# A two-layer decoder trunk on one core: the first four weight tiles side by side, the bias write in four transfers, two small reorderings

## The chip, the cores and the metric

One core of a Trainium2 chip runs the whole program. The metric is device time in microseconds (us). TensorE (PE) multiplies, VectorE (DVE) and ScalarE (ACT) do the elementwise work, SyncE (SP) issues nearly all DMA transfers, GpSimd (POOL) builds a few masks. Engines run their own instruction lists in order and wait for each other by semaphores.

## The reference

x is 512 tokens by 2048. Two layers, each `x = x + mixer(rmsnorm(x))`, then a last rmsnorm.

- Layer 1: one projection gives q, k, v, a gate g (16 heads of 128 each) and a small indexer (16 heads of 64). The indexer scores every causal key, `score = sum_h relu(iq_h . ik) * iw_h`; each query keeps its best 128 keys; softmax attention runs over those, with logits that carry a learned bias by distance (32 buckets per head). The result times `silu(g)` goes through the output projection.
- Layer 2: one projection gives z, x/B/C and dt; a causal convolution of four taps with SiLU; a chunked state-space scan over 64 heads with states carried between chunks of 128 tokens; times `silu(z)`, rmsnorm, output projection.

All matrices are fp32.

## The kernel before

Every dense product keeps fp32 accuracy by three matmuls: a weight block and an activation block are each split into a high part (rounded to fp32r, by ACT: `wh`, `xh`) and a low rest (by DVE: `wl`, `xl`), and PE adds `wh*xh + wh*xl + wl*xh`.

Work is cut into **units**. A dense tile gives 128 output columns; with 2048 input rows it is four units of four blocks of 128 rows, so a unit is 4 steps of three matmuls, twelve in all. The order of everything is written by hand: a main loop goes through the units, and a step counter (`now`, four per unit) wakes generators ("threads") whose `yield n` means "n steps later". Three units (`LEAD`) ahead of PE the loop emits the splits of the coming unit: ACT's `wh` at step 0, DVE's `wl` at step 2. Since every engine works in program order, an instruction that waits holds up all that stands behind it on its engine.

Weights come in transfers of 1 MB, one tile each (`raw<-wa`), into three buffers. `load_next` issues the next one when the last `wl` of a tile has been emitted, which is 12 units before PE needs it. All these loads stand in SP's list, between the small transfers.

The units of layer 1 in order, as the change finds them: the first five indexer tiles `wa[0]` to `wa[4]` (units 0 to 19, quarter by quarter: unit 0 is the first four blocks of tile 0, unit 1 those of tile 1, and so on); indexer tiles 5 to 7 (units 20 to 31); `wai`, the indexer's key (32 to 35); twelve gate tiles g0 to g11 (36 to 83); then v, q and k by heads.

At the start SP issues x's first four blocks and the first quarter of each of the five tiles; ACT issues the rest (`load_early_thread`). `prep_x` splits a block of x. `square_x` sums the squares of x for the first rmsnorm.

`bias_setup` (from unit 40) makes, with one small matmul `r`, a table of 16 heads by 384 distances, 16 partitions high, in the tile `rs`. One transfer then writes each head's row 128 times to a scratch in DRAM, each time one element further on, so that later a skewed read gives each head's bias block (`bias_load`, first used far later, at unit 100):

```
dst = bias_scr.rearrange("h (p m) -> h p m", m=385)[:, :, 0:384]
sy.dma_start(out=dst, in_=rs[:HA, None, :384].to_broadcast([HA, P, 384]))
```

From unit 36 on, `index_thread` puts the indexer's `dots` matmuls between the units, ACT takes their relu, DVE sums them to `score`, and `topk_thread` (DVE, lines 446 and 447) finds the best 128 keys.

`head_thread` does one head's attention: logits for query blocks 3, 2, then 1 and 0 (tiles `la`, `lb`, `lc`; the probabilities of block 0 are in a part of `lb`, scaled last, line 548); then transposes (`ptp`, line 558) in three groups of key blocks, each split by ACT (`pth`) and DVE (`ptl`); then the products with v (`av`).

`pairs_thread` (layer 2) makes the states of two head pairs: `xd2` split by ACT and DVE (`xd2l`), some steps later the six matmuls `st`, then `yo`.

Of the kernel before, what the change touches and what calls it, by code (L numbers as in the profile page):

```python
# [16 lines left out]
P = 128  # L17
# [25 lines left out]
def kernel(  # L43
# [27 lines left out]
    def T(name, dt=F32):  # L71
        return slots.tile([P, S], dt, tag="u", name=name)
# [46 lines left out]

    def cols_load():  # L120
        sy.dma_start(out=cols, in_=cols_in)
        ve.tensor_scalar(out=cols[:, C_CW:C_D], in0=cols[:, C_CW:C_D], scalar1=0.5, scalar2=None, op0=ALU.mult)

    def col(base, k):
# [32 lines left out]
    def spawn(gen, delay=1):  # L157
        threads.append([now[0] + delay, gen])
# [15 lines left out]
    class Dense:  # L174
        def __init__(self, src, ncol, nk, operand, evac, t0=0, t1=S, packed=False, early=None,
                     order=None, keep=(), given=None):
            self.order = list(order or range(nk // 4))
            self.keep, self.given = keep, given
            self.src, self.ncol, self.nk, self.operand, self.evac = src, ncol, nk, operand, evac
            self.t0, self.t1, self.packed, self.early = t0, t1, packed, early  # L180
            self.raw = {}
            self.w = {}

        def load(self, c, eng=sy):
# [3 lines left out]
            n = 4 * self.ncol  # L188
            for u in range(4):
                self.raw[4 * c + u] = r[:, u * n : (u + 1) * n]  # L190

        def load_unit(self, u, eng):
            r = T("rawu")
            eng.dma_start(out=r, in_=self.src[:, 4 * u : 4 * u + 4].rearrange("p k j -> p (k j)"))
            self.raw[u] = r

        def split_hi(self, u):
            n = 4 * self.ncol
# [9 lines left out]
        def split_lo(self, u):  # L208
            if self.given and u in self.given.keep:
                return  # L210
            hi, lo = self.w[u][:2]
            sub(lo, self.raw.pop(u).rearrange("p (k j) -> p k j", k=4), f(hi))
# [24 lines left out]
    class TokenMajor:  # L237
# [21 lines left out]
        def mm(self, u, b):  # L259
# [10 lines left out]
            if u == 15:  # L270
                run(self.evac(out, b))

    tiles = []
    units = []
    hooks = {}

    def dense(src, ncol, nk, operand, evac, **kw):
        d = Dense(src, ncol, nk, operand, evac, **kw)
        tiles.append(d)
        if d.early is None:  # L280
            for u in d.order:
                units.append((d, u))
        return d

    def at_unit(idx, fn):
        hooks.setdefault(idx, []).append(fn)
# [43 lines left out]

    xf, xhl = {}, {}

    def load_x(k, eng):
        xf[k] = T("x")
        eng.dma_start(out=xf[k], in_=xT[k])

    def prep_x(k):
        xhl[k] = yield from split_scaled("x", xf[k], col(C_NW0, k))
# [4 lines left out]
    def square_x():  # L343
        for k in range(KD):
            yield from sum0.push(xf.pop(k))
            yield 1
        yield 4
        yield from rms_chain(sum0.acc, D, True, after_rms0)
# [7 lines left out]
    def bias_setup():  # L356
        rel, oh = T("rel"), T("oh")
        sy.dma_start(out=rel[:32, :HA], in_=rel_in)
        sy.dma_start(out=oh[:32, :384], in_=onehot_in)
        yield 16  # L360
        r = PS("r")
        te.matmul(r[:HA, :384], rel[:32, :HA], oh[:32, :384], start=True, stop=True)
        rs, c0 = T("rs"), SM("c0", 1)
        ve.tensor_copy(out=c0[:HA], in_=r[:HA, 0:1])
        ve.tensor_scalar(out=rs[:HA, :384], in0=r[:HA, :384], scalar1=c0[:HA], scalar2=None, op0=ALU.subtract)
        dst = bias_scr.rearrange("h (p m) -> h p m", m=385)[:, :, 0:384]
        sy.dma_start(out=dst, in_=rs[:HA, None, :384].to_broadcast([HA, P, 384]))

    def bias_load(h):
        b = T("bias")  # L370
# [11 lines left out]
    def evac_iq(t):  # L382
        def go(ps):
            a, b = T("iqa", F32R), T("iqb", F32R)
            for q, h, l in ((a, slice(0, HI), slice(HI, P)), (b, slice(HI, P), slice(0, HI))):
                sc.copy(out=q[h, :384], in_=ps[h])
                yield HOP
                sub(q[l, :384], ps[h], f(q[h, :384]))
            iqhl[t] = (a, b)
        return go  # L390
# [117 lines left out]
    def head_thread(h):  # L508
# [40 lines left out]
            yield 1  # L549
        yield 2  # L550
        pt = {}
        for grp in ((0,), (1,), (2, 3)):
            ps = PS("ptp")
            n = 0
            hi, lo = T("pth", F32R), T("ptl", F32R)
            for j in grp:
                for i in range(j, NB):
                    te.transpose(ps[:, n + (i - j) * P : n + (i - j + 1) * P],  # L558
                                 prob[i][:, j * P : (j + 1) * P], ident)
                w = (NB - j) * P  # L560
                pt[j] = (hi[:, n : n + w], lo[:, n : n + w])
                n += w
            yield 2
            if 3 in grp:

                pt[3] = hi[:, 2 * P :]
                sc.copy(out=hi[:, :n], in_=ps[:, :n])
                yield HOP
                sub(lo[:, : 2 * P], ps[:, : 2 * P], f(hi[:, : 2 * P]))
                sub(hi[:, n:], ps[:, 2 * P : n], f(hi[:, 2 * P : n]))  # L570
            else:
                yield from split(hi[:, :n], lo[:, :n], ps[:, :n])
            yield 1
# [265 lines left out]
    def pairs_thread(p):  # L839
        bth, btl, ch, cl = state_in[p // 4]  # L840
        d2 = T("xd2")
        for e in range(2):
            yield from xdt_make(p + e, d2[:, 256 * e : 256 * e + 256])
        hi, lo = T("xd2h", F32R), T("xd2l", F32R)
        yield from split(hi, lo, d2)
        yield 8
        st = PS("st")[:, :256]
        blk = lambda a, s: a.rearrange("p (e c d) -> p c e d", e=2, c=2)[:, s]
        for s in range(2):
            ss = slice(s * P, (s + 1) * P)  # L850
            te.matmul(st, bth[:, ss], blk(hi, s), start=s == 0, stop=False)
            te.matmul(st, bth[:, ss], blk(lo, s), start=False, stop=False)
            te.matmul(st, btl[:, ss], blk(hi, s), start=False, stop=s == 1)
        sh, sl = T("sth", F32R)[:, :256], T("stl", F32R)[:, :256]
        yield 2
        yield from split(sh, sl, st)
        yield 5
        yo = PS("yo")
        for e in range(2):
            o, es = yo[:, 256 * e : 256 * e + 256], slice(e * P, (e + 1) * P)  # L860
            te.matmul(o, sh[:, es], ch[:, 256:], start=True, stop=False)
            te.matmul(o, sh[:, es], cl[:, 256:], start=False, stop=False)
            te.matmul(o, sl[:, es], ch[:, 256:], start=False, stop=True)
        t = T("yo")
        yield 2
        sc.copy(out=t, in_=yo)
        for e in range(2):
            yoff[p + e] = t[:, 256 * e : 256 * e + 256]
# [189 lines left out]
    def mark():  # L1058
        return len(units)

    EARLY_TILES = 5
    for t in range(8):
        dense(wa[t], P, 16, opA, evac_iq(t), t0=P, early=t if t < EARLY_TILES else None)
        if t == EARLY_TILES - 1:
            for u in range(4):
                for d in tiles:
                    units.append((d, u))
    dense(wai, 80, 16, opA, evac_idx)
    for h in range(12):
        dense(wa[8 + h], P, 16, opA, evac_g(h))  # L1070
# [33 lines left out]
    dense(wbo[KD - 1], P, 32, opO, evac_last(1), t0=256, order=range(7, -1, -1), given=first_half)  # L1104
    u_end = mark()

    at_unit(40, lambda: spawn(bias_setup(), 0))
    at_unit(17, lambda: spawn(square_x(), 0))
    at_unit(u_fill_a, lambda: spawn(og_convert_thread(), 0))
    at_unit(u_out_a - 2, lambda: [res_load(xT, j) for j in range(2)])  # L1110
    at_unit(u_b - 4, lambda: sy.dma_start(out=heads, in_=heads_in))
# [29 lines left out]
    def load_next(eng=sy):  # L1141
        if nxt_chunk[0] < len(chunks):
            d, c = chunks[nxt_chunk[0]]
            d.load(c, eng)
            nxt_chunk[0] += 1

    early = tiles[:EARLY_TILES]

    def load_early(u, eng):
        if u:  # L1150
            early[0].load_unit(u, eng)
        for k in range(4 * u, 4 * u + 4):
            load_x(k, eng)
            if k == 0:
                early[0].load_unit(u, eng)
            yield 1
        for d in early[1:]:
            d.load_unit(u, eng)
            yield 1

    def load_early_thread():
        for u in range(1, 4):
            yield from load_early(u, sc)
            yield 3
        load_next(sc)
        yield 8
        load_next(sc)
        yield 16
        load_next(sc)

    for _ in load_early(0, sy):
        pass

    def prep_x_thread():
        for k in range(4, KD):
            spawn(prep_x(k), 0)
            yield 3

    def split_now(i):
        d, u = units[i]  # L1180
        d.split_hi(u)
        d.split_lo(u)

    x0 = prep_x(0)
    next(x0)
    d0, u0 = units[0]
    d0.split_hi(u0)
    for _ in x0:
        pass
    d0.split_lo(u0)  # L1190
    for k in range(1, 4):
        for _ in prep_x(k):
            pass
    for i in range(1, LEAD):
        split_now(i)
    spawn(load_early_thread(), 0)
    spawn(prep_x_thread(), 3)
    at_unit(12, cols_load)

    for i in range(u_end):  # L1200
        j = i + LEAD
# [81 lines left out]
```

## Time and profile before

| | |
|---|---|
| device time, median of 3 runs | 2418.91 us (2417.77 to 2419.24) |
| the profiled execution's own time | 2418.09 us |
| span of its profile | 2416.4 us |
| PE busy | 2399.8 us, 99% |
| PE weight loads busy | 2016.2 us, 83% |
| DVE busy | 1582.5 us, 65% |
| ACT busy | 1072.4 us, 44% |
| granted PE clock | 0.999 of full speed |

The span runs from the first instruction to the last; 1.7 us of the execution's own time lie outside it. Matmuls are pipelined, so a matmul shown as 0.39 us follows the one before it after 0.23 us; a short wait shows as a longer distance between two starts rather than as idle time.

### The profile page before, as it was taken

To read this page: it belongs to the slowest core of one execution; us is meant where nothing else is said; L and a number is where in the kernel's file an instruction comes from. 1 tells how busy PE (TensorE), PEld (TensorE's weight loads), DVE (VectorE), ACT (ScalarE), POOL (GpSimd) and SP (SyncE) were. 2 spreads that over 40 slices of the span, in tenths; PEclk is the share of its full clock that TensorE was granted. 3 is DMA by queue.
4 is the path that set the end of the run, shared out by engine and by line. 5 is a ranking of instruction groups with operands and counts; after the bars stand their busy time and mean duration, and the time that the engine had idled before them with its cause. 6 is when DMAs were issued, how large, how long until landed. Compare 5 with 4: busy or idle time off the path is not lost.

```text
span 2416.4 us, 29873 instructions
## 1 busy us (share of the span) xinstructions
PE 2399.8 (99%) x11398; PEld 2016.2 (83%) x11398; DVE 1582.5 (65%) x2891; ACT 1072.4 (44%) x2134; POOL 1.2 (0%) x8
## 2 busy tenths in 40 slices
PE   9999999999999999999999999999999999999998
PEld 9878888888888888888888888888888888888887
DVE  6569466464654654358788888888888888433334
ACT  6433233333333433234556565565656566322222
POOL 0000000000000000000000000000000000000000
PEclk9999999999999999999999999999999999999999
DMA  6362322222222224433333333333334344333333
GB/s 223 103 130 88 107 93 74 92 90 90 94 79 93 82 105 142 146 122 130 122 108 119 118 122 126 127 127 106 124 107 142 112 149 157 127 114 100 101 113 109
DMA packets 83440, 278.54 MB, mean 115 GB/s; under 512 B 7744, under 2 KB 40928, under 8 KB 58208
## 3 DMA queue, kind: packets, MB, share of 16 engines
q1 hardware_dynamic: 78976, 266.41, 33.0%
q10 hardware_dynamic: 4320, 10.23, 1.2%
q8 instruction: 89, 1.46, 0.3%
q14 instruction: 55, 0.45, 0.1%
HBM read 258.32 MB, written 18.02 MB: 114 GB/s over the span
## 4 chain that ended last, share of the span: by engine, by line
PE 96%; DVE 2%; DMA 2%; issue 0%; ACT 0%; SPq 0%; DVEq 0%; ACTq 0%
PE acc L229 27%; PE acc L231 27%; PE acc L230 27%; PE acc L265 2%; PE acc L267 2%; PE acc L266 2%; DMA raw<-wa 2%; PE ptp L558 1%; PE y L917 1%; PE y L916 1%; PE xst L819 1%; PE sps L525 0%; PE sps L526 0%; PE sps L524 0%; PE av L588 0%; PE av L586 0%
## 5 line engine op out<-in xcount | busy, mean ns | idle before, releaser
L90 DVE TENSOR_TENSOR wl<-raw,wh 128x512 fp32r<-128x512 f32 (+1 forms) x788 | 528.7, 684 | 136.8 <-ACT wh L206 96.2
L206 ACT CAST wh<-raw 128x512 fp32r<-128x512 f32 (+1 forms) x724 | 427.0, 613 | 173.9 <-PE acc L230 100.1
L229 PE MATMUL acc<-x1h,wh 128*128 128x512 f32 x1280 | 503.4, 393 | 0.0
L230 PE MATMUL acc<-x1l,wh 128*128 128x512 f32 x1280 | 499.5, 390 | 0.0
L231 PE MATMUL acc<-x1h,wl 128*128 128x512 f32 x1280 | 499.2, 390 | 0.0
L229 PE MATMUL acc<-xh,wh 128*128 128x512 f32 (+2 forms) x912 | 353.5, 388 | 2.3 <-ACT wh L206 2.1
L231 PE MATMUL acc<-xh,wl 128*128 128x512 f32 (+2 forms) x912 | 349.6, 383 | 0.3
L230 PE MATMUL acc<-xl,wh 128*128 128x512 f32 (+2 forms) x912 | 348.8, 382 | 0.6 <-DVE xl L101 0.6
L231 PEld LDWEIGHTS acc<-x1h,wl 128*128 128x128 f32 x1280 | 240.4, 188 | 50.9
L229 PEld LDWEIGHTS acc<-x1h,wh 128*128 128x128 f32 x1280 | 240.8, 188 | 46.6
L230 PEld LDWEIGHTS acc<-x1l,wh 128*128 128x128 f32 x1280 | 240.9, 188 | 46.1
L229 PE MATMUL acc<-ygh,wh 128*128 128x512 f32 (+1 forms) x544 | 205.4, 378 | 0.0
L231 PE MATMUL acc<-ygh,wl 128*128 128x512 f32 (+1 forms) x544 | 205.0, 377 | 0.0
L230 PE MATMUL acc<-ygl,wh 128*128 128x512 f32 (+1 forms) x544 | 205.0, 377 | 0.0
L231 PEld LDWEIGHTS acc<-xh,wl 128*128 128x128 f32 (+1 forms) x912 | 170.6, 187 | 35.1 <-DVE wl L90 2.2
L229 PEld LDWEIGHTS acc<-xh,wh 128*128 128x128 f32 (+1 forms) x912 | 170.7, 187 | 31.8 <-ACT wh L206 2.6
L230 PEld LDWEIGHTS acc<-xl,wh 128*128 128x128 f32 (+1 forms) x912 | 171.0, 187 | 29.8 <-DVE xl L101 1.4
L231 PEld LDWEIGHTS acc<-ygh,wl 128*128 128x128 f32 x544 | 102.4, 188 | 18.8
L230 PEld LDWEIGHTS acc<-ygl,wh 128*128 128x128 f32 x544 | 102.4, 188 | 18.7
L229 PEld LDWEIGHTS acc<-ygh,wh 128*128 128x128 f32 x544 | 102.4, 188 | 18.5
L727 DVE SCALAR_TENSOR_TENSOR hh<-rw,cols,hh 128x511 f32<-128x511 f32 x144 | 107.4, 746 | 6.5 <-ACT hh L724 4.0
L887 ACT ACTIVATE bc<-bc,aloc 128x256 f32<-128x256 f32 (+1 forms) x256 | 102.8, 446 | 0.5
(295 smaller groups left out, 3316.1 us busy)
## 6 DMA issues: line engine op xcount, KB each, us to landing
raw<-wb SPq DMA_DIRECT2D x80, 1024.0 KB, 4.9
raw<-wa SPq DMA_DIRECT2D x48, 1024.0 KB, 4.9
raw<-wbo SPq DMA_DIRECT2D x33, 1024.0 KB, 4.8
bc<-r_scr SPq DMA_DIRECT2D x96, 256.0 KB, 6.1
raw<-wav SPq DMA_DIRECT2D x16, 1024.0 KB, 4.9
raw<-wao SPq DMA_DIRECT2D x16, 1024.0 KB, 5.4
yg_scr<-yy SPq DMA_DIRECT2D x24, 256.0 KB, 4.6
ygr<-yg_scr SPq DMA_DIRECT2D x24, 256.0 KB, 5.1
```

The lines of the kernel that those rows point to most:

```text
L90: ve.tensor_tensor(out=out, in0=a, in1=b, op=ALU.subtract)
L206: sc.copy(out=self.w[u][0], in_=self.raw[u].rearrange("p (k j) -> p k j", k=4))
L229: te.matmul(out[:m], w[0], xh[:, ts], start=first, stop=False)
L230: te.matmul(out[:m], w[0], xl[:, ts], start=False, stop=False)
L231: te.matmul(out[:m], w[1], xh[:, ts], start=False, stop=last)
L265: te.matmul(out, xh[:, bs], wh, start=u == 0, stop=False)
L266: te.matmul(out, xh[:, bs], wl, start=False, stop=False)
L267: te.matmul(out, xl[:, bs], wh, start=False, stop=u == 15)
L558: te.transpose(ps[:, n + (i - j) * P : n + (i - j + 1) * P], prob[i][:, j * P : (j + 1) * P], ident)
L727: ve.scalar_tensor_tensor(out=hh[:, d:], in0=rw[:, : S - d], scalar=col(C_CW, 4 * ct + 3 - d), in1=hh[:, d:], op0=ALU.mult, op1=ALU.add)
L819: te.transpose(ps[:, c * P : (c + 1) * P], xs[p][:, c * P : (c + 1) * P], ident)
L887: sc.activation(out=t3[:, e, a:b], in_=t3[:, e, a:b], func=AF.Relu, scale=-1.0, bias=aloc[:, s, 2 * p + e : 2 * p + e + 1])
```

## The change

Four things change.

1. The first four tiles are worked side by side (`FourTiles`). A unit is now one block of 128 rows of x against that block of all four tiles, so units 0 to 15 hold four tiles; the fifth tile becomes an ordinary one. SP issues all early loads, x block by x block: for the first four blocks a transfer of 128 partitions x 4 tiles x 128 columns (rows of 512 B), after that for four blocks at once, 1 MB (rows of 2 KB). ACT issues none. The number of units stays the same.
2. `bias_setup` starts four units earlier, and its write goes in four transfers of four heads, 24 steps (6 units) apart.
3. A head's transposes are done for key blocks (2, 3), then 1, then 0, instead of 0, 1, (2, 3).
4. The `st` matmuls come 10 steps after the split of `xd2`, not 8.

The loading of `cols` moves into the row of early loads, and its scaling to unit 20; `square_x` starts at unit 13, not 17.

```diff
+    class FourTiles:
+        def load(self, k):
+            load_x(k)
+            if k < 4:
+                self.raw[k] = T("rawu").rearrange("p (t j) -> p t j", t=4)
+                sy.dma_start(out=self.raw[k], in_=self.src[:4, :, k].rearrange("t p j -> p t j"))
+            elif k % 4 == 0:
+                r = raw_pool.tile([P, 16 * P], F32, tag="raw", name="raw").rearrange("p (t k j) -> p t k j", t=4, k=4)
+                sy.dma_start(out=r, in_=self.src[:4, :, k : k + 4].rearrange("t p k j -> p t k j"))
...
+        def split_hi(self, k):
+            self.x = prep_x(k)
+            next(self.x)
+            self.w[k] = [T("wh", F32R), T("wl", F32R)]
+            sc.copy(out=self.cut(self.w[k][0]), in_=self.raw[k])
...
+        def mm(self, k, t):
+            if k == 0 and t == 0:
+                self.acc = [PS("acc4")[:, : S - self.t0] for _ in range(4)]
...
+            te.matmul(self.acc[t], wh, xh, start=k == 0, stop=False)
+            te.matmul(self.acc[t], wh, xl, start=False, stop=False)
+            te.matmul(self.acc[t], wl, xh, start=False, stop=k == KD - 1)
...
@@ bias_setup
-        sy.dma_start(out=dst, in_=rs[:HA, None, :384].to_broadcast([HA, P, 384]))
+        for g in range(4):
+            hs = slice(4 * g, 4 * g + 4)
+            sy.dma_start(out=dst[hs], in_=rs[hs, None, :384].to_broadcast([4, P, 384]))
+            yield 24
@@ head_thread
-        for grp in ((0,), (1,), (2, 3)):
+        for grp in ((2, 3), (1,), (0,)):
@@ pairs_thread
-        yield 8
+        yield 10
...
-    at_unit(40, lambda: spawn(bias_setup(), 0))
-    at_unit(17, lambda: spawn(square_x(), 0))
+    at_unit(36, lambda: spawn(bias_setup(), 0))
+    at_unit(13, lambda: spawn(square_x(), 0))
...
+    for k in range(KD):
+        first.load(k)
+        if k == 11:
+            cols_load()
+    for _ in range(3):
+        load_next()
```

Where instructions stand now, at three places. First, SP's list at the bias write; `raw` is the next 1 MB weight tile (here the gate tiles g4, g5 and so on). Before:

```order
L187 DMA raw_1100<-wa 128x2048
L367 DMA bias_scr_118<-rs_1196 2048x1x384
L187 DMA raw_1211<-wa 128x2048
L187 DMA raw_1314<-wa 128x2048
L187 DMA raw_1424<-wa 128x2048
```

With the change:

```order
L414 DMA bias_scr_118<-rs_1057 512x1x384
L189 DMA raw_1083<-wa 128x2048
L189 DMA raw_1187<-wa 128x2048
L414 DMA bias_scr_118<-rs_1057 512x1x384
L189 DMA raw_1291<-wa 128x2048
L414 DMA bias_scr_118<-rs_1057 512x1x384
L189 DMA raw_1402<-wa 128x2048
L189 DMA raw_1530<-wa 128x2048
L414 DMA bias_scr_118<-rs_1057 512x1x384
L189 DMA raw_1658<-wa 128x2048
```

The one write of 2048 rows stood behind the load for g4 (raw_1100) and ahead of that for g5. Now four writes of 512 rows stand ahead of the loads for g4 (raw_1083), g6 (raw_1291), g7 (raw_1402) and g9 (raw_1658).

Second, PE's list at the transposes of the last head (la, lb and lc hold the probabilities). Before:

```order
L558 MATMUL ptp_7550<-ident_95,lb_7309 128x128
L558 MATMUL ptp_7550<-ident_95,lc_7310 128x128
L558 MATMUL ptp_7550<-ident_95,lb_7309 128x128
L558 MATMUL ptp_7550<-ident_95,la_7308 128x128
...
L586 MATMUL av_7664<-pth_7551,vh_6374 128x512
L587 MATMUL av_7664<-ptl_7552,vh_6374 128x512
```

With the change:

```order
L606 MATMUL ptp_7529<-ident_95,lb_7288 128x128
L606 MATMUL ptp_7529<-ident_95,la_7287 128x128 x2
...
L606 MATMUL ptp_7588<-ident_95,lb_7288 128x128
L606 MATMUL ptp_7588<-ident_95,lc_7289 128x128
L606 MATMUL ptp_7588<-ident_95,lb_7288 128x128
L606 MATMUL ptp_7588<-ident_95,la_7287 128x128
...
L634 MATMUL av_7643<-pth_7589,vh_6353 128x512
L635 MATMUL av_7643<-ptl_7590,vh_6353 128x512
```

The first group needed all four query blocks, block 0's part of lb among them; now it needs blocks 2 and 3 alone, and the group that needs all four comes last, just ahead of the product with v that reads it (ptp_7588 is split into pth_7589 and ptl_7590).

Third, SP's list at the very start (`rawu` is the weight data of one early unit). Before:

```order
L118 DMA nw_93<-cols 128x16
L335 DMA x<-xT 128x512
L194 DMA rawu<-wa 128x512
L335 DMA x<-xT 128x512 x3
L194 DMA rawu<-wa 128x512 x4
```

With the change:

```order
L118 DMA nw_93<-cols 128x16
L380 DMA x<-xT 128x512
L283 DMA rawu<-wa 128x4x128
L380 DMA x<-xT 128x512
L283 DMA rawu<-wa 128x4x128
L380 DMA x<-xT 128x512
L283 DMA rawu<-wa 128x4x128
```

x and weights now alternate, block by block, and a weight transfer has 512 rows of 512 B where it had 128 rows of 2 KB.

## Rows read from the trace of the kernel before

**Rows 1.** The page: the span and the engines' busy time.

```profile
span 2416.4 us, 29873 instructions
PE 2399.8 (99%) x11398; PEld 2016.2 (83%) x11398; DVE 1582.5 (65%) x2891; ACT 1072.4 (44%) x2134; POOL 1.2 (0%) x8
```

**Rows 2.** The waits of PE over the whole span: who was waited for, us in total, times, longest. The three rows left out are the warm-up at the start (1.1) and two of 0.3 and 0.2 us.

```profile
PE acc L229 <- ACT wh L206: 2.1, 2, 1.7
PE st L852 <- DVE xd2l L90: 1.1, 1, 1.1
...
PE ptp L558 <- DVE lb L548: 1.1, 1, 1.1
PE acc L230 <- DVE xl L101: 0.6, 2, 0.3
...
```

**Rows 3.** The timeline of PE (start us, duration, operation, idle before it and its releaser) where the kernel loses time: around the late gate tile, the last head's first transpose, and one `st`.

```profile
150.07 0.34 PE L425 MATMUL dots<-iklb,iqb 128*128 128x384 f32 x1
152.08 0.51 PE L229 MATMUL acc<-xh,wh 128*128 128x512 f32 x1 [1.67 <-ACT wh L206]
...
862.15 0.39 PE L231 MATMUL acc<-xh,wl 128*128 128x512 f32 x1
863.60 0.33 PE L558 MATMUL ptp<-ident,lb 128*128 128x128 f32 x1 [1.06 <-DVE lb L548]
...
1248.53 0.28 PE L851 MATMUL st<-xd2h,bth 128*128 128x256 f32 x1
1249.95 0.39 PE L852 MATMUL st<-xd2l,bth 128*128 128x256 f32 x1 [1.15 <-DVE xd2l L90]
```

**Rows 4.** The timeline of PE at the start: the first dense matmul, the fourth (7.33) and the thirteenth (10.64), after which they follow each other without a wait.

```profile
6.32 0.44 PE L229 MATMUL acc<-xh,wh 128*128 128x384 f32 x1 [0.42 <-ACT wh L206]
7.33 0.34 PE L229 MATMUL acc<-xh,wh 128*128 128x384 f32 x1
10.64 0.34 PE L229 MATMUL acc<-xh,wh 128*128 128x384 f32 x1
```

**Rows 5.** The chain of waits from 110 to 175 us: the piece that the load of g5 makes up, and the two splits that end it.

```profile
114.39 36.99 DMA raw<-wa
151.41 0.62 ACT wh L206
152.06 0.69 DVE wl L90
```

**Rows 6.** SP's timeline around the bias write, and the small matmul that goes ahead of it on PE's.

```profile
111.95 0.82 PE L362 MATMUL r<-oh,rel 32*16 32x384 f32 x2
...
113.64 0.66 SPq L367 DMA_DIRECT2D bias_scr<-rs  x1
114.39 82.45 SPq L187 DMA_DIRECT2D raw<-wa  x7
```

**Rows 7.** Stretches (from:to, length, busy time and instructions of PE, its weight loads, DVE, ACT and POOL, granted clock, DMA share, GB/s). The DMA share is the mean busy share of the 16 DMA engines. The stretches are: early loads in rows of 2 KB, 1 MB weight loads into 128 partitions, the bias write, the writes of `scan` out of 64 partitions in rows of 1 KB and of 512 B, and a stretch of top-k work.

```profile
22.00:24.00 2.00, 2.00 (x14) 2.00 (x13) 0.89 (x3) 1.61 (x3) 0.00 (x0) 1.00 1.05 395
36.00:38.00 2.00, 2.00 (x14) 2.00 (x13) 1.43 (x3) 0.00 (x0) 0.00 (x0) 1.00 1.00 410
130.00:135.00 5.00, 5.00 (x25) 4.17 (x25) 2.41 (x5) 1.33 (x4) 0.00 (x0) 1.00 0.91 99
1114.40:1114.90 0.50, 0.50 (x4) 0.42 (x3) 0.50 (x3) 0.50 (x2) 0.00 (x0) 1.00 0.59 131
1115.00:1115.40 0.40, 0.40 (x4) 0.32 (x3) 0.40 (x2) 0.05 (x1) 0.00 (x0) 1.00 0.37 82
200.00:250.00 50.00, 50.00 (x222) 41.45 (x221) 48.48 (x102) 20.73 (x38) 0.00 (x0) 1.00 0.26 90
```

**Rows 8.** The page: DMA issues by kind (count, KB each, median us from issue to landing).

```profile
bias_scr<-rs SPq DMA_DIRECT2D x1, 3072.0 KB, 33.5
raw<-wa SPq DMA_DIRECT2D x48, 1024.0 KB, 4.9
```

**Rows 9.** The timeline of PE: the first matmul of unit 40, and the first low-part matmul (line 231, the third matmul) of units 60, 64 and 72, the first units of the gate tiles g6, g7 and g9.

```profile
99.33 0.50 PE L229 MATMUL acc<-xh,wh 128*128 128x512 f32 x1
166.04 0.50 PE L231 MATMUL acc<-xh,wl 128*128 128x512 f32 x1
179.31 0.39 PE L231 MATMUL acc<-xh,wl 128*128 128x512 f32 x1
206.06 0.39 PE L231 MATMUL acc<-xh,wl 128*128 128x512 f32 x1
```

**Rows 10.** The timelines of DVE and PE: at the last two heads, the end of the last transposed group's split (`ptl`, `pth`) and the first `av` after it, with block 0's last scaling (863.26); and one ordinary state, `xd2l` against `st`.

```profile
850.10 0.28 DVE L90 TENSOR_TENSOR pth<-ptp,pth 128x128 fp32r<-128x128 f32 x1
850.39 0.39 PE L586 MATMUL av<-pth,vh 128*128 128x512 f32 x1
863.26 0.29 DVE L548 TENSOR_SCALAR lb<-lb,sm 128x128 f32<-128x128 f32 x1
874.87 0.28 DVE L90 TENSOR_TENSOR pth<-ptp,pth 128x128 fp32r<-128x128 f32 x1
877.13 0.39 PE L586 MATMUL av<-pth,vh 128*128 128x512 f32 x1
...
1358.02 0.69 DVE L90 TENSOR_TENSOR xd2l<-xd,xd2h 128x512 fp32r<-128x512 f32 x1
1361.28 0.28 PE L852 MATMUL st<-xd2l,bth 128*128 128x256 f32 x1
```

More of the change, by code (lines that the diff above doesn't have):

```diff
@@ L121, in cols_load, with scale_cols @@
         sy.dma_start(out=cols, in_=cols_in)
+    def scale_cols():
         ve.tensor_scalar(out=cols[:, C_CW:C_D], in0=cols[:, C_CW:C_D], scalar1=0.5, scalar2=None, op0=ALU.mult)
@@ L190, in load @@
                 self.raw[4 * c + u] = r[:, u * n : (u + 1) * n]
[L192 to L195, printed above, removed]
         def split_hi(self, u):
@@ L271, in mm, with __init__, split_lo, cut @@
                 run(self.evac(out, b))
+    class FourTiles:
+        given, early, nk = None, True, 64
+        def __init__(self, src, evacs, t0):
+            self.src, self.evacs, self.t0 = src, evacs, t0
+            self.raw, self.w = {}, {}
+        def load(self, k):
[6 more added lines that the diff above has]
+                sy.dma_start(out=r, in_=self.src[:4, :, k : k + 4].rearrange("t p k j -> p t k j"))
+                for i in range(4):
+                    self.raw[k + i] = r[:, :, i]
+        def split_hi(self, k):
[3 more added lines that the diff above has]
+            sc.copy(out=self.cut(self.w[k][0]), in_=self.raw[k])
+        def split_lo(self, k):
+            for _ in self.x:
+                pass
+            hi, lo = self.w[k]
+            sub(self.cut(lo), self.raw.pop(k), f(self.cut(hi)))
+        def cut(self, w):
+            return w.rearrange("p (t j) -> p t j", t=4)
+        def mm(self, k, t):
+            if k == 0 and t == 0:
+                self.acc = [PS("acc4")[:, : S - self.t0] for _ in range(4)]
+            wh, wl = [a[:, t * P : (t + 1) * P] for a in self.w[k]]
+            xh, xl = [a[:, self.t0 :] for a in xhl[k]]
+            te.matmul(self.acc[t], wh, xh, start=k == 0, stop=False)
+            te.matmul(self.acc[t], wh, xl, start=False, stop=False)
+            te.matmul(self.acc[t], wl, xh, start=False, stop=k == KD - 1)
+            if t == 3:
+                del self.w[k]
+            if k == KD - 1:
+                run(self.evacs[t](self.acc[t]))
     tiles = []
@@ L331, with load_x @@
     xf, xhl = {}, {}
-    def load_x(k, eng):
+    def load_x(k):
         xf[k] = T("x")
-        eng.dma_start(out=xf[k], in_=xT[k])
+        sy.dma_start(out=xf[k], in_=xT[k])
     def prep_x(k):
@@ L1059, in mark @@
         return len(units)
[L1061 to L1067, printed above, removed]
+    first = FourTiles(wa, [evac_iq(t) for t in range(4)], P)
+    for k in range(KD):
+        units.append((first, k))
+    for t in range(4, 8):
+        dense(wa[t], P, 16, opA, evac_iq(t), t0=P)
     dense(wai, 80, 16, opA, evac_idx)
@@ L1145, in load_next @@
             nxt_chunk[0] += 1
[L1147 to L1177, printed above, removed]
     def split_now(i):
@@ L1182, in split_now @@
         d.split_lo(u)
[L1184 to L1194, printed above, removed]
+    for k in range(KD):
+        first.load(k)
[3 more added lines that the diff above has]
+        load_next()
+    for i in range(LEAD):
         split_now(i)
-    spawn(load_early_thread(), 0)
-    spawn(prep_x_thread(), 3)
-    at_unit(12, cols_load)
+    at_unit(20, scale_cols)
     for i in range(u_end):
```

## The prediction

> **What bounds the kernel now.** I read the page first: PE is busy 2399.8 of 2416.4 us [rows 1]. Such a kernel can gain only where PE waits, and it loses whatever makes PE wait. So the next view is the list of PE's waits [rows 2]. It is short: ACT's `wh` 2.1 us, a state `st` 1.1, a transpose `ptp` 1.1, the split of x at the start 0.6. Third, the timeline at these places, since a wait shows less as idle time than as distance between starts. A matmul of 384 columns is followed by the next after 0.17 us, one of 512 after 0.23, one of 256 after 0.12. So the late gate tile costs 152.08 - 150.07 - 0.17 = 1.84 us, the transpose 863.60 - 862.15 - 0.23 = 1.22, the state 1249.95 - 1248.53 - 0.12 = 1.30 [rows 3]. At the start the thirteenth dense matmul comes at 10.64; from the fourth, at 7.33, on without waits it would come at 7.33 + 9 x 0.173 = 8.89, so 1.75 us are lost [rows 4]. After the late tile some 0.7 us more go in small waits up to 170 us, which I count with it: 2.5.
>
> The chain of waits tells what made the tile late: the load of g5 took 36.99 us from issue to landing, and 1.31 us of splits follow [rows 5], where a load usually lands in 4.9 [rows 8]. It was issued at 114.39, right behind the bias write at 113.64 [rows 6], which took 33.5 us [rows 8]. A transfer on SP's queue thus waits for the one ahead.
>
> **The change, part by part.**
>
> *Transposes.* The group that waited (for `lb`, ready at 863.55) moves two groups later, some 7 us, and the first group needs only what has long been there. Gain 1.2 us. The price could be the last group's split, which `av` now reads first: its end is 2.0 us ahead of `av` in the last head and 0.01 us in the one before [rows 10]. There the new split is one of 512 in place of 256 and 128, much the same time, and only the second `av` matmul needs it, 0.23 us later. I take 0; at worst 0.2.
>
> *States.* Two steps are 6 matmuls, 1.36 us, against 1.30 lost: gain 1.25. Elsewhere `xd2l` (1358.02 + 0.69) is 2.6 us ahead of `st` [rows 10], so nothing else changes; `yo` moves along by the same two steps. At worst, 0.
>
> *Start.* A block now needs one x and one weight transfer of 256 KB each for 12 matmuls, 2.08 us of PE. At 395 GB/s [rows 7] they take 0.66 us each, so PE would be ahead of nothing: the full 1.75 us would be won. The first four weight transfers have rows of 512 B. The nearest row, rows of 512 B out of 64 partitions, moves 82 GB/s at a share of 0.37, so 222 GB/s at full share, or 1.18 us [rows 7]; then the first 1 MB transfer lands four times 0.52 us later and PE meets it about 0.2 us behind the old schedule. Bounds +1.75 and -0.2; I take 1.0, between them, since the same view gives 131/0.59 = 222 for rows of 1 KB too, so the row's length is not what slows that one. [...]
>
> *The bias write in four.* This decides. The old write moves 3,145,728 bytes at 99 GB/s while the engines are 91% busy, where 1 MB loads move 410 at the same share [rows 7]: the engines are there, but each is slowed by four. Its 16 source rows lie in 16 partitions. Out of 64 partitions the same view gives 222 GB/s per full share, out of 16 it gives 99/0.91 = 109, into 128 it gives 410. The fewer partitions, the slower. A piece reads 4 partitions, each 128 times as before. Bounds for a piece of 786,432 bytes: 7.9 us, if 99 GB/s hold for 4 partitions too, and 31.6 us, if the rate goes down with the partitions to a quarter (24.9 GB/s). I take 31.6: the old write is slow by a limit that four partitions, or the engine that reads a partition, share, and each partition of a piece still has its 128 rows to give.
>
> [...]
>
> Now the queue. The order on SP is p1, g4, g5, p2, g6, p3, g7, g8, p4, g9, each issued long before the one ahead ends, so they run end to end. Unit 40 starts at 99.33 [rows 9] less the 1.0 of the start, 98.3; from the small matmul `r` to the issue it was 1.7 us [rows 6], and about 1.1 more to the first bytes: p1 starts at 101.1. A load is 1 MB at 410 GB/s, 2.56 us. Landing and the two splits take 2.0 [rows 5]. PE can then use:
> - g6 (unit 60) at 101.1 + 2 x 31.6 + 3 x 2.56 + 2.0 = 174.0, where without waits it would come at 166.04 - 3.5 = 162.5: wait 11.5;
> - g7 (unit 64) at 101.1 + 3 x 31.6 + 4 x 2.56 + 2.0 = 208.1, where it would come 13.3 us after unit 60, at 187.3: wait 20.8;
> - g9 (unit 72) at 101.1 + 4 x 31.6 + 6 x 2.56 + 2.0 = 244.9, where it would come 26.8 us after unit 64, at 234.9: wait 10.
>
> Unit 72 came at 206.06 [rows 9]. It comes 38.8 us later; the start and the old stall are in this already. While DVE waits, the work behind `wl` on its list (scores and top-k, `zr` of the gates) waits too, and DVE is 97% busy there afterwards [rows 7], so I add 0.7, what such a backlog cost last time. The scratch is first read at unit 100, long after.
>
> *Nothing:* `square_x`, `cols`, the loads moved off ACT: ACT has half its time free.
>
> **Sum**, against the profiled execution: 2418.1 + 38.8 + 0.7 - 1.2 - 1.25 = 2455.1. The median lies 0.8 higher than that execution: I predict 2455.
>
> **Rivals.**
> - *No stall: faster.* The pieces take about 8 us, or each sits on engines of its own; g6 then has 162.5 - 2 to land in and does so. It wins 1.0 + 2.5 + 1.2 + 1.25 = 6.0 us: 2412.9. For it: the old write used all 16 engines, and a limit of 99 GB/s on writing short odd-placed rows would look the same. Against it: the rates out of 64 and 16 partitions. It decides at the length of a piece: unit 72 is met in time (202.5) up to (202.5 - 101.1 - 15.4 - 2.0)/4 = 21 us. Chance 0.19.
> - *No stall, but the start loses* 0.2 instead of winning 1.0, by the 1.18 us above: 2414.1, or 2415 with a split that comes late for `av`. Chance 0.06; unchanged.
> - *Half-way.* A piece takes 21 to 27 us: each us above 21 costs four. At 25: unit 72 at 218.5, so 2418.9 + 12.4 + 0.7 - 2.45 = 2429.6. Chance 0.05.
> - *The forecast*, 0.70, with its own range 2436 (27 us a piece) to 2463 (32 us and some 6 us of further waits of the DVE backlog).
>
> A measurement of this kernel can tell 0.2%, 4.8 us, from no change. Faster by more: 0.15 of the first rival and 0.01 half-way, 0.16. Same: 0.04 of the first, all of the second, 0.10. Slower: 0.74. To leave out no more than 2 in 10 the range must reach down to the first rival: 2411 to 2463.
>
> **What the profile after would show.** Right: four `bias_scr` issues, the median to landing over 30 us; loads of 30 us and more behind them; PE's waits for `wh`, `wl` near 174, 208 and 245 us, over 30 us in sum, DVE idle just before; `ptp` and `st` gone from PE's waits; the thirteenth dense matmul before 10 us. Wrong: bias pieces that land in about 10 us, loads near 5 beside them, and PE without waits from 10 to 850 us.

## The result and the profile after

The changed kernel takes 2448.2 us (median; 2447.9 to 2449.0), the kernel before 2418.7: ratio 1.0123, 95% interval 1.0109 to 1.0138. 2455 was forecast. The profiled execution took 2448.99 us; its span is 30.5 us longer than that of [rows 1].

The page of the changed kernel:

```profile
span 2446.9 us, 29833 instructions
PE 2405.5 (98%) x11398; PEld 2020.1 (83%) x11398; DVE 1581.2 (65%) x2891; ACT 1069.3 (44%) x2134; POOL 1.2 (0%) x8
```

PE's waits over the whole span, all of them (who was waited for, us in total, times, longest):

```profile
PE acc L226 <- ACT wh L203: 29.5, 4, 16.0
PE warm L109 <- DVE ones L106: 1.1, 1, 1.1
PE acc L310 <- ACT wh L294: 0.5, 1, 0.5
PE bc L1087 <- DVE r L359: 0.3, 1, 0.3
```

Beside [rows 2], the waits for `ptp` and `st` are gone, and `wh` has grown from 2.1 us to 29.5. In PE's timeline: the first and the thirteenth dense matmul, as in [rows 4]; then the waits, at the first matmul of units 60, 64 and 72, with a few behind the second that show the distance between neighbours:

```profile
6.04 0.42 PE L310 MATMUL acc<-xh,wh 128*128 128x384 f32 x1
...
8.95 0.45 PE L310 MATMUL acc<-xh,wh 128*128 128x384 f32 x1 [0.46 <-ACT wh L294]
...
170.71 0.79 PE L226 MATMUL acc<-xh,wh 128*128 128x512 f32 x1 [7.86 <-ACT wh L203]
...
201.94 0.80 PE L226 MATMUL acc<-xh,wh 128*128 128x512 f32 x1 [16.02 <-ACT wh L203]
202.54 0.63 PE L227 MATMUL acc<-xl,wh 128*128 128x512 f32 x1
202.96 0.63 PE L228 MATMUL acc<-xh,wl 128*128 128x512 f32 x1
...
206.56 0.39 PE L226 MATMUL acc<-xh,wh 128*128 128x512 f32 x1
206.79 0.39 PE L227 MATMUL acc<-xl,wh 128*128 128x512 f32 x1
...
236.36 0.79 PE L226 MATMUL acc<-xh,wh 128*128 128x512 f32 x1 [5.35 <-ACT wh L203]
```

The thirteenth comes at 8.95, for 10.64 before; the forecast was under 10.

SP's timeline over the four pieces (start, how long the issuing instruction held SP; a row x2 runs from the start of the first of two issues to the end of the second):

```profile
99.68 0.79 SPq L414 DMA_DIRECT2D bias_scr<-rs  x1
100.63 13.02 SPq L189 DMA_DIRECT2D raw<-wa  x2
113.71 3.72 SPq L414 DMA_DIRECT2D bias_scr<-rs  x1
125.35 18.38 SPq L189 DMA_DIRECT2D raw<-wa  x1
143.79 3.76 SPq L414 DMA_DIRECT2D bias_scr<-rs  x1
147.65 31.05 SPq L189 DMA_DIRECT2D raw<-wa  x2
178.75 3.75 SPq L414 DMA_DIRECT2D bias_scr<-rs  x1
182.60 31.68 SPq L189 DMA_DIRECT2D raw<-wa  x2
```

And stretches (columns as in [rows 7]): two during the first piece, and two after the long wait:

```profile
102.00:110.00 8.00, 8.00 (x40) 6.75 (x39) 3.29 (x6) 2.57 (x7) 0.00 (x0) 1.00 0.23 25
110.00:112.00 2.00, 2.00 (x11) 1.68 (x10) 0.39 (x1) 0.49 (x1) 0.00 (x0) 1.00 0.77 147
...
202.00:205.00 3.00, 3.00 (x7) 2.38 (x8) 3.00 (x6) 2.96 (x7) 0.00 (x0) 0.50 0.24 62
206.00:209.00 3.00, 3.00 (x14) 2.48 (x13) 2.93 (x8) 2.37 (x5) 0.00 (x0) 0.96 0.23 25
```

While a piece runs alone the DMA engines are busy at 0.23, about four of sixteen, and move 25 GB/s; the one write of before stood at 0.91 and 99 [rows 7]. By the trace's packets a row of 1536 B takes 0.225 us in the first piece and took 0.227 in the old write (medians): a row costs the same, but only four engines carry rows (in the first piece no more than four rows are under way at once). The pieces run from 101.06 to 132.85, 137.29 to 167.15, 168.88 to 198.46 and 202.12 to 232.86. The row at 110:112 (0.77, 147 GB/s) shows the load for g4 going on beside a piece, on the twelve free engines; its last quarter, 32 of 128 packets, has to wait on the other four and lands at 135.80. g6, g7 and g9 land at 169.96, 201.25 and 235.66.

The start of a unit (its first low-part matmul), less the same in the kernel before, adds up the loss and the gains:

| unit | 24 | 50 | 58 | 60 | 62 | 64 | 66 | 72 | 74 | 200 | after the heads | after the first states |
|---|---|---|---|---|---|---|---|---|---|---|---|---|
| us | -0.97 | -1.16 | -2.54 | +5.69 | +6.91 | +23.65 | +25.24 | +31.32 | +32.77 | +33.12 | +31.82 | +30.46 |

### The profile page after: what moved, and what is told of

Same layout as the page of the kernel before. It is cut to its first block, busy times and chain, and to the rows that moved or that the text cites. A ratio compares the mean times of both kernels' runs of the same rounds, so it can differ in the third digit from the quotient of the medians.

```text
span 2446.9 us, 29833 instructions
## 1 busy us (share of the span) xinstructions
PE 2405.5 (98%) x11398; PEld 2020.1 (83%) x11398; DVE 1581.2 (65%) x2891; ACT 1069.3 (44%) x2134; POOL 1.2 (0%) x8
## 4 chain that ended last, share of the span: by engine, by line
PE 94%; DMA 3%; another core or an unknown queue 1%; DVE 1%; ACT 0%; issue 0%; SPq 0%; DVEq 0%; ACTq 0%
PE acc L226 26%; PE acc L228 26%; PE acc L227 26%; DMA raw<-wa 3%; PE acc L262 2%; PE acc L264 2%; PE acc L263 2%; PE ptp L606 1%; PE y L965 1%; PE y L964 1%; PE xst L867 1%; PE acc L312 0%; PE acc L310 0%; PE acc L311 0%; PE sps L573 0%
## 5 line engine op out<-in xcount | busy, mean ns | idle before, releaser
L90 DVE TENSOR_TENSOR wl<-raw,wh 128x512 fp32r<-128x512 f32 x804 | 539.7, 684 | 186.0 <-ACT wh L203 143.0
L203 ACT CAST wh<-raw 128x512 fp32r<-128x512 f32 x728 | 429.4, 613 | 224.9 <-PE acc L227 99.9
L226 PE MATMUL acc<-xh,wh 128*128 128x512 f32 (+2 forms) x848 | 334.0, 394 | 29.5 <-ACT wh L203 29.5
L228 PE MATMUL acc<-xh,wl 128*128 128x512 f32 (+2 forms) x848 | 329.4, 388 | 0.0
L227 PE MATMUL acc<-xl,wh 128*128 128x512 f32 (+2 forms) x848 | 328.8, 388 | 0.0
L226 PEld LDWEIGHTS acc<-xh,wh 128*128 128x128 f32 (+1 forms) x848 | 159.9, 189 | 59.6 <-ACT wh L203 31.2
L228 PEld LDWEIGHTS acc<-xh,wl 128*128 128x128 f32 (+1 forms) x848 | 159.6, 188 | 34.5 <-DVE wl L90 1.7
L227 PEld LDWEIGHTS acc<-xl,wh 128*128 128x128 f32 (+1 forms) x848 | 160.2, 189 | 28.7
```

What stands on the lines that cost most here:

```text
L90: ve.tensor_tensor(out=out, in0=a, in1=b, op=ALU.subtract)
L203: sc.copy(out=self.w[u][0], in_=self.raw[u].rearrange("p (k j) -> p k j", k=4))
L226: te.matmul(out[:m], w[0], xh[:, ts], start=first, stop=False)
L227: te.matmul(out[:m], w[0], xl[:, ts], start=False, stop=False)
L228: te.matmul(out[:m], w[1], xh[:, ts], start=False, stop=last)
```

## Experiments

Two theories: four neighbouring partitions share one limit of some 25 GB/s, whatever engines read them; or an engine needs 0.225 us for such a row wherever it reads, and a piece is slow only because it is on four engines. Both give the same trace above.

**Is the bias write the whole loss?** One run takes the split back, one puts it alone into the kernel before.

```diff
-        for g in range(4):
-            hs = slice(4 * g, 4 * g + 4)
-            sy.dma_start(out=dst[hs], in_=rs[hs, None, :384].to_broadcast([4, P, 384]))
-            yield 24
+        sy.dma_start(out=dst, in_=rs[:HA, None, :384].to_broadcast([HA, P, 384]))
```

> The changed kernel with the bias write in one transfer of 16 heads again (still from unit 36). If the four pieces are the whole loss, everything else of the change stays won: unit 58 stands 2.5 us ahead of the kernel before in the changed kernel's trace, the transposes give 1.3, the states 1.4, so 2418.1 - 5.2 = 2412.9 (2412 to 2414.5), one wait below 1 us for the gate tile g4 near 137 us, none at 170, 200 and 235. If the order of the early loads or of the heads has a share in the loss, 2420 or more.

2412.8 us, ratio 0.9975 (0.9965 to 0.9985), as expected. PE waits once for g4, 0.6 us.

The loop above in the kernel before, with nothing else:

> The kernel before with only the bias write in four (from unit 40, as there). By pieces of 30.5 us end to end with 1.7 to 4.4 us of loads between them, the first from 114.8: g7 (unit 64) can be used at 185 (wait 6), g8 (68) at 217 (wait 17), g10 (76) at 251 (wait 7), and about 1.5 us more behind each; unit 76 at 252.5 where it was at 219.2, 2418.7 + 32 = 2451 (2447 to 2454). If the early loads or their order are needed for the loss, 2419.

2453.3 us, ratio 1.0143 (1.0129 to 1.0157). The first row of PE's waits is

```profile
PE acc L229 <- ACT wh L206: 30.8, 4, 16.9
```

The loss is the split's, with or without the rest.

**Partitions or engines?** Three ways to cut, each in four transfers of the same size at the same steps. By rows, all 16 heads in each:

```diff
-            hs = slice(4 * g, 4 * g + 4)
-            sy.dma_start(out=dst[hs], in_=rs[hs, None, :384].to_broadcast([4, P, 384]))
+            ps = slice(32 * g, 32 * g + 32)
+            sy.dma_start(out=dst[:, ps], in_=rs[:HA, None, :384].to_broadcast([HA, 32, 384]))
```

> Four pieces again, at the same steps and of the same size, but each writes 32 rows of all 16 heads, so reads 16 partitions. Theory: the loss is in what a piece reads (four neighbouring partitions), not in there being four transfers. Then a piece takes a quarter of 33 us, about 8, and the time is 2412 to 2414, without a wait for wh over 1 us between 120 and 260 us. Rival: four transfers of this write cost 30 us each however cut (their issue, their completions): 2448.

2410.8 us, ratio 0.9967 (0.9955 to 0.9980): the shortest median of all runs, better than both kernels, and below the 2412 to 2414 that I expected. Against the one write (2412.8) it wins 2.0 us; 1.1 us of that lie between units 50 and 52, where PE waits for g4 behind the one write. A piece takes 5.7 to 8.1 us. A stretch of the first piece, with nearly all engines busy again:

```profile
101.00:108.00 7.00, 7.00 (x35) 5.87 (x34) 3.44 (x8) 2.62 (x6) 0.00 (x0) 1.00 0.92 104
```

By heads, but every fourth, then every second of eight:

```diff
-            hs = slice(4 * g, 4 * g + 4)
+            hs = slice(g, HA, 4)
```

> Each piece still has four heads, but every fourth one, so its four partitions are not neighbours (0, 4, 8, 12 in the first). Partition theory: the four neighbours share one limit of 25 GB/s; apart they don't, a row takes well under 0.227 us, a piece under 15 us, and the time is 2412 to 2416. Engine theory: an engine needs 0.227 us for each row of this write wherever it reads, and a piece is on four engines: 30 us a piece as in the changed kernel, 2446 to 2450.

```diff
-            hs = slice(4 * g, 4 * g + 4)
+            hs = slice(8 * (g // 2) + g % 2, 8 * (g // 2) + 8, 2)
```

> Each piece has every second head of eight: 0, 2, 4, 6, then 1, 3, 5, 7, and so on, so two of its partitions lie in each of two groups of four neighbours. Four engines again. If a group of four neighbours is the limit, at 1536 bytes in 0.225 / 4 = 0.056 us, two engines share one group and a row takes 0.112 us, a piece 128 x 0.112 = 14.4 us: below the 21 us from which the forecast let pieces cost anything, so no wait and 2411 to 2412.5. If neighbouring pairs, or groups of eight, were the limit: 0.072 us (9 us a piece), or 0.225 us (30 us, 2448).

2411.1 us (0.9969, 0.9957 to 0.9981) and 2411.0 (0.9969, 0.9957 to 0.9980); PE waits for no weights in either. A stretch of every fourth with a piece alone, and one of every second:

```profile
130.20:138.50 8.30, 8.30 (x40) 6.98 (x39) 4.29 (x9) 3.18 (x7) 0.00 (x0) 1.00 0.27 94
```

```profile
110.00:111.50 1.50, 1.50 (x9) 1.25 (x9) 0.58 (x1) 0.00 (x0) 0.00 (x0) 1.00 0.24 48
```

All three cuts by heads keep a quarter of the engines busy (0.23, 0.24 and 0.27), and move 25, 48 and 94 GB/s: partitions in one, two and four groups of neighbours. A row takes 0.225, 0.122 and 0.072 us, a piece 30 to 32, 15 to 17 and 9 us. The engine theory falls; the limit belongs to the four neighbours. With four engines on four groups a row takes 0.072 us and not 0.056, a quarter of 0.225, so there something else sets it; no run here tells what. The limit also fits the old write, where a row took as long as in a piece (0.227 us): its sixteen partitions lie in four groups, so sixteen engines are four to a group there too, and its 99 GB/s [rows 7] are 25 to a group. The split by neighbours left three groups and twelve engines idle.

**Does a piece cost by itself, or only end to end?**

```diff
-            yield 24
+            yield 56
```

> The changed kernel with its four neighbouring-head pieces 56 steps (14 units, some 44 us) apart instead of 24 (6 units, 19 us). A piece still takes 30 us, but the next begins after the queue has emptied. If the loss is pieces end to end, each load late by more than the one before: a load that is delayed by one piece alone came 0.7 us late in the changed kernel (g4) and the others have as much time, so 2411 to 2415. If every piece costs a wait by itself: 2430 to 2448.

2411.4 us, ratio 0.9970 (0.9959 to 0.9981), with pieces of 29 to 32 us: 101.5 to 133.2, 145.9 to 175.7, 183.2 to 212.4, 232.3 to 261.8. No weight load after the start is left in the list of PE's waits. By the starts of the units the first piece costs 0.6 us (units 50 to 52) and the other three nothing. So a slow transfer alone costs little; four in a row use up the time by which loads are ahead.

**Queue or engines?** ACT issues the pieces:

```diff
-            sy.dma_start(out=dst[hs], in_=rs[hs, None, :384].to_broadcast([4, P, 384]))
+            sc.dma_start(out=dst[hs], in_=rs[hs, None, :384].to_broadcast([4, P, 384]))
```

> The changed kernel, its four neighbouring-head pieces issued by ACT instead of SP, so that no load stands behind one in its queue. If the loads lose by standing behind a piece: a load meets the piece only on four of its engines, whose other rows are 2 KB at 0.084 us; turn by turn with rows of 0.227 us its 32 rows there take about 10 us, the loads land in some 12 us in place of 30, PE doesn't wait, 2411 to 2414. If an engine finishes the piece before it takes the load's rows, loads land after 30 us as before: 2448. A third way: ACT's list is held up at the issue as SP's was (3.7 us a piece), its splits come late: 2414 to 2425.

2453.5 us, ratio 1.0143 (1.0129 to 1.0157): outside all I wrote for the first and the third way, and not for the second's reason. Loads beside a piece did land sooner, 9 to 18 us after their issue (18 for g4, 9 for g5, 17 for g6, 18 for g7). But ACT was held at the third and fourth issue, and DVE waited for a piece itself:

```profile
134.47 14.10 ACTq L414 DMA_DIRECT2D bias_scr<-rs  x1
...
160.78 18.93 ACTq L414 DMA_DIRECT2D bias_scr<-rs  x1
```

```profile
DVE score L479 <- DMA bias_scr<-rs: 30.5, 1, 30.5
PE acc L228 <- DVE wl L90: 25.9, 3, 23.8
```

In that kernel a `score` tile takes over the buffer of `rs`, which the last piece was still reading; `wl` stands behind it on DVE. So this run moved the loss. What sharing the engines costs it tells for one load, g4, which came before ACT was held: it landed 17.8 us after its issue and PE lost nothing (units 50 and 54 both stand 1.64 us ahead of the kernel before). That is more than the 12 us I had expected; my estimate took the load's rows for 2 KB at 0.084 us and let one row of the piece go by for each. In the trace the load has packets of 8 KB at 0.309, 8 to an engine, and 276 rows of the piece went by on its four engines until it had landed, some nine to a packet. The next has POOL issue them, and `rs` in a buffer of its own:

```diff
+    own = ctx.enter_context(tc.tile_pool(name="own", bufs=1))
...
-        rs, c0 = T("rs"), SM("c0", 1)
+        rs, c0 = own.tile([P, 384], F32, tag="rs", name="rs"), SM("c0", 1)
...
+            gp.dma_start(out=dst[hs], in_=rs[hs, None, :384].to_broadcast([4, P, 384]))
```

> The changed kernel, its four neighbouring-head pieces issued by POOL, which does nothing else there, and with a buffer of its own for rs, so that neither ACT's list nor a tile that takes over rs's place waits for a piece. If both were what made the run with ACT's queue slow, and sharing four engines alone costs a load only 10 to 15 us: 2411 to 2414, loads landing 9 to 18 us after their issue. If sharing is what costs: 2440 or more. POOL's issues have no row in any trace here; if they come late the scratch is still read only at unit 100.

2411.2 us, ratio 0.9970 (0.9957 to 0.9982). But these are not the same transfers. POOL issued all four at once, and the DMA share then is no quarter:

```profile
99.61 4.44 POOL L415 DMA_DIRECT2D bias_scr<-rs  x4 [97.44 <-DVE iwc L460]
```

```profile
110.00:120.00 10.00, 10.00 (x49) 8.38 (x48) 5.97 (x11) 3.67 (x9) 0.00 (x0) 1.00 0.96 122
```

From POOL three rows go as one packet of 4608 B, and all sixteen engines work, at 0.96: the four pieces together ended 47 us after the first issue. From SP the second piece, issued at 113.71, began only at 137.29, behind the first, though the share from 120 to 130 was 0.23. Why the pieces from SP stay on four engines and those from POOL don't, no run here tells. Loads landed 5 to 24 us after their issue, in time. What PE would lose if all four slow pieces shared four engines with the loads from another queue, with nothing else late, stays open; g4 above is the one case.

**The rest of the change.** The two reorderings alone, and everything but the early tiles (the kernel before with the reorderings and the bias write by rows):

```diff
-        for grp in ((0,), (1,), (2, 3)):
+        for grp in ((2, 3), (1,), (0,)):
...
-        yield 8
+        yield 10
```

> The kernel before with only the two reorderings: transposes (2, 3), 1, 0 and the states two steps later. If they are worth what the trace of the changed kernel shows (1.3 and 1.4 us): 2418.7 - 2.7 = 2416.0 (2415 to 2417). If what they win there is only a part of the time that PE stood still earlier: 2418.7.

> The kernel before with the two reorderings and the bias write in four pieces by rows (16 partitions each), from unit 40 as before: everything of the change, mended, but the early tiles side by side. The reorderings give 2.7, the late gate tile 2.5: 2418.7 - 5.2 = 2413.5 (2412.5 to 2414.5). The difference to the changed kernel mended by rows, 2410.8, is what the early tiles side by side win: 1.0 by the forecast would make this 2411.8; 2.7 us if the first matmuls of the kernel before also come later by 1.2 in most runs.

2415.9 us (ratio 0.9987, 0.9978 to 0.9996) and 2413.2 (0.9976, 0.9967 to 0.9984). The reorderings are worth 3.2 us by the medians (2419.1 for the kernel before beside them; 2.7 in the trace); the gate tile that is no longer late, 2.7 (2415.9 - 2413.2); the early tiles side by side, with what moved along (`cols`, `square_x`, the earlier start of `bias_setup`), some 2.4 (2413.2 - 2410.8, of two series in which the kernel before stood at 2419.1 and 2418.7).

## Why the prediction was right, and where it was off

The direction, the mechanism and the place were right, and 2448.2 lies in the range 2411 to 2463: 29.5 us slower than before, where 36 were forecast. The range reaches down to the first rival, so that the time lies in it says little; that the mechanism was right is shown by the pieces of 30 us and the waits behind them. By its own steps:

- *Piece length.* 31.6 us was taken, the upper bound; the four took 31.8, 29.9, 29.6 and 30.7. The first began at 101.06, for 101.1. The forecast left open whether partitions or the engine set it. No row of the kernel before shows that four partitions share a limit: it was an estimate then, and the 25, 48 and 94 GB/s out of one, two and four groups of neighbours show it.
- *End to end.* Right, but the pieces, with the loads between them, took less room than forecast: 36.2, 31.6 and 33.2 us from start to start, for 36.7, 34.2 and 36.7, and the last piece 30.7 for 31.6. So g9 could be used at 237.4, not 244.9, and unit 72 came 31.3 us later than before, not 38.8; this is the term that was mis-sized. The loads are the smaller part of it: one costs each of the four engines 8 packets of 8 KB at 0.309 us, 2.47 us, for the 2.56 taken. The larger part lies in the pieces: 47 to 55 rows at the start of each of the later three took 0.065 us in place of 0.225, by an estimate from these numbers 2 us a piece on four engines. Why these rows are quick stays open. I had also let the issues cost nothing. SP was held for 9 to 28 us at a load behind a piece; the loads between two pieces still took no more than 1.7 to 4.4 us, so that cost nothing here.
- *The waits* were forecast at 11.5, 20.8 and 10 us at units 60, 64 and 72. By the table they are 8.2 (5.69 + 2.54), 16.7 and 6.1, and 0.7 at unit 52, which I hadn't listed. 29.5 in the list of waits is less: the table goes by the third matmul of a unit, and after each long wait that came 1.02 us behind the first, for some 0.46 otherwise.
- *After the wait*, 0.7 us for a backlog on DVE. What was lost is 1.45 us from unit 72 to 74, where PE's clock was down to 0.50 (below), and 0.3 more up to unit 82. At units 60 and 64 the same loss, 1.2 and 1.6, is swallowed by the next wait, whose end the pieces set.
- *Transposes* -1.2: measured -1.3 (+33.1 to +31.8). *States* -1.25: measured -1.4. The end of the last split, which I feared for `av`, cost nothing.
- *Start* -1.0: -0.97 against the profiled execution, by luck in part. In the three other profiled runs with the old start unit 24 comes 0.9 to 1.8 us later than in the kernel before's profile; in the eight with the new start 0.5 to 1.7 earlier. Against a typical run it wins about 2.2 (the means of four and of eight profiles), so the one profile I worked from had a quick start. On the bounds: a row of 512 B took its engine 0.027 us (median of the 2048), a row of 2 KB 0.084. By these a weight transfer of 256 KB in rows of 512 B needs an estimated 0.86 us on sixteen engines, between the 0.66 and 1.18 of the two bounds; rows of 512 B moved at 19 GB/s to an engine here, rows of 2 KB at 24.

With the measured terms: 2418.1 + 31.3 + 1.8 - 1.3 - 1.4 = 2448.5, for 2449.0 in the profiled execution.

The first rival, no stall and 2412.9, is what the kernel does once a piece is short: 2410.8 to 2411.1, with 1.9 us more than I gave it, most of it the start. That pieces cost nothing up to 21 us agrees with 15 to 17 us in the run with every second head; 21 itself was not tried.

## What to carry to other kernels

When a small table in SBUF is written many times to DRAM, count the groups of four neighbouring partitions that a transfer reads (25, 48 and 94 GB/s out of one, two and four here), and cut it along another axis than the partitions, or so that each piece still reads from every group: 16 heads by 32 rows took 6 to 8 us a piece, every fourth head by 128 rows 9, four neighbouring heads by 128 rows 30 for the same bytes. A slow transfer in the queue of the loads did little harm as long as the loads' lead was longer and the next one came after the queue had emptied (one of 32 us cost 0.6 to 0.7 us here; four end to end cost 37, 2448.2 against 2411.4 with the same four apart). Before you move it to another engine's queue, look at who then waits: in ACT's queue the wait moved to ACT's list, and to DVE, which got the source's buffer next.

## What the hardware showed beyond that

After PE had stood still for 16 us, its granted clock was 0.50 (202 to 205): matmuls of 512 columns then followed each other after 0.43 us, from 206.56 on again after 0.23, at 0.96. The waits of 7.9 and 5.4 us were followed by the same, 0.50 from 171 to 174 and from 238 to 240. In the kernel before, the wait of 1.67 us [rows 3] had no such tail: the granted clock was 1.00 from 152 to 155, and from 153.14 on matmuls came 0.23 us apart.

```profile
152.00:155.00 3.00, 2.92 (x12) 2.19 (x13) 2.87 (x9) 3.00 (x8) 0.00 (x0) 1.00 0.62 259
```

So a long wait of PE cost more than it lasted here: 0.56 us in the first three matmuls (1.02 - 0.46), and 1.2 to 1.6 us behind them.

An issuing instruction was not always free: SP was held at a load for up to 28 us behind a piece (31.68 us for two issues in its timeline), and ACT for 14 and 19 us at the third and fourth piece. The first load behind a piece, issued right after it at 100.63, was held for 9.2 us; with the pieces wide apart a load issued 9 us into one, at 154.88, held SP for 0.33.
